# A diffusion layer in one program: fewer unread products at the start, a list that counts a half clock, another start of the buffer ring, and a new table of shifts

## The chip, the cores and the metric

The kernel runs on one core of a Trainium2 chip. Its engines are TensorE (PE, matrix products into the banks of PSUM), VectorE (DVE), ScalarE (ACT), GpSimd (POOL) and SyncE (SP, which issues nearly all DMAs). They run side by side, each working through its own list of instructions in order, and wait for each other through semaphores. The metric is the device time of one execution in microseconds (us).

## The reference

One layer over 512 latent tokens and 256 context tokens, model width 1024, all in float32:

```python
mod = silu(c) @ w_ada + b_ada                 # and the same from c_ctx, for the context
h  = rms_norm(x, g_norm1) * (1 + sc1) + sh1   # hc from ctx likewise
aq, ak, av, dq, dk, dv, dz, da, db, ga, gd = split_cols(h @ w_in)
y_attn = window_ctx_attention(q_a, k_a, v_a, k_ac, v_ac, attn_sink)
o_dc, s_cf, s_cb = bidir_delta(context inputs, zero states)    # gated delta rule, chunks of 64
o_dl, _, _ = bidir_delta(latent inputs, s_cf, s_cb)            # both directions, 8 heads of 64
y_d = rms_norm(o_dl, dn_norm_g) * silu(dz)
y = sigmoid(ga) * (y_attn @ w_br_attn) + sigmoid(gd) * (y_d @ w_br_dn)
x = x + gt1 * (y @ w_out)
x = x + gt2 * (square(relu(hm @ w_mlp1)) @ w_mlp2)             # hm: modulated norm of x
```

In a chunk of the delta rule a unit lower triangular system of 64 x 64 is solved (here by inverting its blocks), and a state of 64 x 64 per head and direction goes from chunk to chunk.

## The kernel before

Activations lie with features on the 128 partitions and tokens along the free axis, so 1024 features are 8 tiles. A product in float32 precision is mostly made of three products in a rounded format (`fp32r`): value and weight are each split into a rounded part (`hi`, ACT) and the rest (`lo`, DVE), and `mm3` (lines 331, 333, 335) adds hi*hi, hi*lo and lo*hi. Plain float32 products take two passes of PE and stand in a trace as two records.

The stages, in the order of time:

- **The front.** `ones` is a 128 x 128 tile of ones. Line 230 multiplies it with itself `NONES` times; nobody reads the result. x is loaded in four pieces (line 260); `norm_x` squares them (ACT, line 402), adds halves (DVE, 404 and 405) and sums over the features with the `ones` tile (PE, 406); then Ln and Exp on ACT (line 185) give 1/rms. Ln needs another table of functions than the Silu of c before it; line 181 loads a table. `ada` (line 249, tiles of 128 x 32) multiplies Silu(c) with 16 loads of 512 KB of `w_ada`, `columns` (267, 272, 281, 282) makes of it scale and shift of one feature tile, and `features` (339 to 341) the modulated input of that tile. Three projections begin at once on what is there (`early_x`, `early_c`). Lines 276 and 434 are further unread products, of `NWAIT` and `WARM`.
- **Projections, attention, inversion.** Weights come by DMA into a ring of `NWR` = 2 raw buffers (`wr`) and are split by lines 295 and 300 into `wh` and `wl` (`wload`, `wnext`). Softmax is at lines 657 to 746, the inversion and its last products at 894 and 993 to 1004 and, for the output, 1395 to 1407.
- **The scan** (`chain_step`, products of 64 x 64 at line 1243, DVE at 1256 to 1324), two directions in turn. Between its steps PE gets products that are independent of it: the gate tiles (line 1148) and the attention branch (1194).
- **The end of the scan.** DVE scales the output by its norm (line 1439), PE turns it back with 16 transposes (1444), DVE applies the gate (1449), lines 224 and 225 split it, and the DeltaNet branch, output projection and MLP follow in `mm3` and at line 1612.
- **The late condition weights** (`late_mod`, lines 508 and 511): 32 loads of 512 KB of `w_ada`, each summed on DVE against the row `scr_`, placed by hand between scan and MLP.

Work buffers come from one ring (`Arena`), whose pointer goes on with each `alloc`; an `alloc` that is freed at once (`NSKIP` times, line 506 before) only moves the pointer. Which buffer an `alloc` gets decides whose old readers its first writer waits for.

The order of each engine's instructions is made by a list scheduler inside the kernel (`arrange`, `Lists.run`): it goes through all instructions with a cost for each (`Step.cost`: time on the engine, time to the result), takes for each engine the ready instruction of lowest rank, and fixes the order that comes out. A rank is the place in the program plus the shifts of the table `SHIFTS` (engine or -1 for all, first, end, places). These costs set the order alone.

Of the kernel before, what the change touches and what calls it, by code (L numbers as in the profile page):

```python
# [29 lines left out]
NONES, NWAIT = 30, 8  # L30
# [7 lines left out]
NSKIP = 2  # L38
WARM = (0, 3, 3, 3, 2, 0, 0, 0)
NROWS = 2  # L40
ND1 = 3
NGD = 5
P = 128
# [8 lines left out]
HC = CH // 2  # L52
# [65 lines left out]
def tile_layer(ctx: ExitStack, tc: tile.TileContext, I: dict, out: bass.AP, dbg=None):  # L118
# [277 lines left out]
    def norm_x():  # L396
        ss = bank()
        for i in range(4):
# [7 lines left out]
            PE.matmul(ss.ap, ones, b[:, :512], start=(i == 0), stop=(i == 3))  # L406
            b.free()
        act(rx, ss.ap, AF.Ln, bias=epsc, scale=1.0 / D)
# [1343 lines left out]
class Step:  # L1752
# [39 lines left out]
    def cost(self):  # L1792

        n = self.cols
        if self.kind == "InstMatmult":
            if self.dtype.endswith("32r"):
                return (226 if n == 512 else max(60, 7 + .44 * n)), n * .44 + 175
            if self.dtype.endswith("16"):
                return 96, 240
            if self.whole:  # L1800
                return (110, 280) if self.ins.is_transpose else (max(62, 1.72 * n), max(62, 1.72 * n) + 170)
            return (142, 300) if self.tile[0] == P else (30 if self.tile[1] > HC else 19, 220)
# [78 lines left out]
class Lists:  # L1881
# [27 lines left out]
    def run(self, rank):  # L1909
# [30 lines left out]
        for _ in range(n):  # L1940
# [26 lines left out]
            else:  # L1967
                own, lag = self.cost[k]
                if e == 0:
                    words, had = words + self.words[k], words  # L1970
# [12 lines left out]
            for x in after[k]:  # L1983
                if x >= n:
                    at = end + 40
                elif eng[x] == e and not self.dma[k]:
                    at = free[e] if e == 0 else end + 10
                else:
                    at = end + note[eng[x]]
# [144 lines left out]
```

## Time and profile before

| | |
|---|---|
| median of 3 runs | 871.31 us (870.93 to 871.32) |
| the profiled execution | 871.5 us |
| its span (first to last instruction) | 869.7 us |
| PE busy | 852.3 us |
| DVE busy | 647.0 us |
| ACT busy | 498.4 us |
| DMA | 106.86 MB, mean 123 GB/s |

A row of the trace gives the start in us from the span's start, the duration in us, engine, line, operation, the tiles by the program's names (buffer numbers left out; out<-in) and, in brackets, the idle time before it and what ended it. "x16" means that many records in a row. The end of a matmul is modelled, so a row's duration is longer than its step to the next start.

### The profile page before, as it was taken

The page shows a single profiled execution, that of the slowest core. Times are in us where ns is not written, and L with a number is a line of the kernel's source. Part 1 is how long each engine was busy: PE and PEld are TensorE (multiplying, and loading weights), DVE is VectorE, ACT ScalarE, POOL GpSimd, SP SyncE. Part 2 cuts the span into 40 slices and gives each one's busy share as a digit, 9 for nine tenths or more (in the row PEclk, how much of TensorE's full clock was granted, in tenths as well). Part 3 has the DMA queues.
Part 4 walks back from the last instruction along what each step waited for, and adds up shares of the span by engine and source line. Part 5 has one row for each costly group of instructions (what it writes and reads, how often), then busy time and mean ns, then how long its engine had stood idle before and what let it go on. Part 6 is the DMA issues. An engine that isn't in the chain of part 4 may idle for free.

```text
span 869.7 us, 17973 instructions
## 1 busy us (share of the span) xinstructions
PE 852.3 (98%) x7544; PEld 712.8 (82%) x7544; DVE 647.0 (74%) x1113; ACT 498.4 (57%) x882; POOL 26.1 (3%) x42
## 2 busy tenths in 40 slices
PE   9999999999999999899999999999999999999998
PEld 6688778877777778677778899888998899889986
DVE  4865899987779997867848969993876478648741
ACT  5567875487669886587754435552555256415620
POOL 0000001010000002000000000000000000000000
PEclk9999999999999999999999999999999999999999
DMA  9924465533121236733116744743412332342031
GB/s 365 352 72 98 88 134 122 120 76 70 38 38 31 68 131 212 243 99 100 40 54 220 264 144 131 249 139 121 146 33 74 122 140 70 97 128 92 26 121 49
DMA packets 31986, 106.86 MB, mean 123 GB/s; under 512 B 4001, under 2 KB 4513, under 8 KB 31905
## 3 DMA queue, kind: packets, MB, share of 16 engines
q1 hardware_dynamic: 29600, 97.33, 33.6%
q0 software_dynamic: 2304, 8.39, 6.2%
q8 instruction: 59, 0.97, 0.5%
q14 instruction: 23, 0.18, 0.1%
HBM read 103.61 MB, written 2.10 MB: 122 GB/s over the span
## 4 chain that ended last, share of the span: by engine, by line
PE 77%; DVE 9%; ACT 6%; DMA 6%; issue 2%; SPq 0%; ACTq 0%; DVEq 0%
PE banks L331 14%; PE banks L333 14%; PE banks L335 14%; PE banks L1612 14%; PE banks L1148 7%; DMA m<-in_wada 3%; PE banks L1243 3%; PE banks L1194 3%; ACT m L185 2%; PE banks L725 1%; DVE wl L300 1%; DMA wr<-in_win 1%; PE banks L781 1%; DVE m L511 1%; DMA wr<-in_wbr 1%
## 5 line engine op out<-in xcount | busy, mean ns | idle before, releaser
L331 PE MATMUL banks<-m,wh 128*128 128x512 f32 (+1 forms) x568 | 210.7, 374 | 2.2 <-ACT m L224 1.3
L333 PE MATMUL banks<-m,wh 128*128 128x512 f32 (+1 forms) x568 | 211.2, 372 | 0.0
L335 PE MATMUL banks<-m,wl 128*128 128x512 f32 (+1 forms) x568 | 209.9, 370 | 0.1
L295 ACT ACTIVATE wh<-wr 128x1024 fp32r<-128x1024 f32 (+1 forms) x92 | 90.4, 984 | 128.3 <-PE banks L333 82.7
L331 PEld LDWEIGHTS banks<-m,wh 128*128 128x128 f32 x568 | 107.0, 189 | 20.4 <-ACT m L224 1.5
L1612 PEld LDWEIGHTS banks<-m,m 128*128 128x128 f32 x1008 | 122.2, 192 | 0.7
L335 PEld LDWEIGHTS banks<-m,wl 128*128 128x128 f32 x568 | 106.9, 188 | 19.2 <-issue 1.0
L1612 PE MATMUL banks<-m,m 128*128 128x256 f32 x1008 | 122.4, 283 | 0.0
L333 PEld LDWEIGHTS banks<-m,wh 128*128 128x128 f32 x568 | 107.1, 188 | 18.1 <-issue 0.7
L224 ACT ACTIVATE m<-m 128x512 fp32r<-128x512 f32 (+2 forms) x118 | 82.4, 721 | 66.1 <-PE banks L1612 14.9
L1148 PE MATMUL banks<-m,wh 128*128 128x512 f32 x320 | 104.1, 402 | 1.8 <-ACT m L185 1.0
L225 DVE TENSOR_TENSOR m<-m,m 128x512 fp32r<-128x512 f32 (+2 forms) x118 | 92.3, 804 | 15.5 <-ACT m L224 13.9
L300 DVE TENSOR_TENSOR wl<-wr,wh 128x1024 fp32r<-128x1024 f32 (+1 forms) x76 | 84.3, 1109 | 17.1 <-ACT wh L295 14.6
L1739 DVE SCALAR_TENSOR_TENSOR m<-banks,modT,m 128x512 f32<-128x512 f32 x32 | 24.0, 749 | 65.0 <-PE banks L335 64.9
L1148 PEld LDWEIGHTS banks<-m,wh 128*128 128x128 f32 x320 | 58.6, 188 | 14.4 <-ACT m L185 1.4
L1148 PE MATMUL banks<-m,wl 128*128 128x512 f32 x160 | 63.7, 400 | 0.4 <-DVE wl L300 0.4
L331 PE MATMUL banks<-m,m 128*128 128x256 f32 (+1 forms) x136 | 45.5, 340 | 0.4 <-ACT m L295 0.3
L333 PE MATMUL banks<-m,m 128*128 128x256 f32 (+1 forms) x136 | 45.6, 342 | 0.1
L511 DVE SCALAR_TENSOR_TENSOR m<-m,m 128x1024 f32<-128x1024 f32 x32 | 39.1, 1222 | 8.4 <-DMA m<-in_wada 8.2
L335 PE MATMUL banks<-m,m 128*128 128x256 f32 (+1 forms) x120 | 40.2, 337 | 0.0
L1243 PEld LDWEIGHTS banks<-m,m 64*64 64x64 f32 x1600 | 26.7, 134 | 12.5 <-issue 4.3
L1148 PEld LDWEIGHTS banks<-m,wl 128*128 128x128 f32 x160 | 30.0, 188 | 7.3 <-DVE wl L300 1.1
(263 smaller groups left out, 1313.7 us busy)
## 6 DMA issues: line engine op xcount, KB each, us to landing
m<-in_wada SPq DMA_DIRECT2D x48, 512.0 KB, 4.8
wr<-in_wm SPq DMA_DIRECT2D x40, 512.0 KB, 3.6
wr<-in_win SPq DMA_DIRECT2D x38, 512.0 KB, 3.7
m<-in_wm SPq DMA_DIRECT2D x24, 512.0 KB, 3.7
wl<-in_win POOLq DMA_DIRECT2D x16, 512.0 KB, 5.8
m<-in_xT SPq DMA_DIRECT2D x8, 512.0 KB, 5.9
wr<-in_wbr SPq DMA_DIRECT2D x16, 256.0 KB, 2.7
wr<-in_wout SPq DMA_DIRECT2D x8, 512.0 KB, 4.4
```

The lines of the kernel that those rows point to most:

```text
L224: A.activation(r32(hi), src, AF.Copy)
L225: (eng or V).tensor_tensor(r32(lo), src, hi, op=ALU.subtract)
L295: upper[0] = A.activation(r32(hi), raw, AF.Copy)
L300: V.tensor_tensor(r32(lo), raw, hi, op=ALU.subtract)
L331: PE.matmul(acc, w[0][:, k, :], xhi, start=(start and i == 0), stop=False)
L333: r = PE.matmul(acc, w[0][:, k, :], xlo, start=False, stop=(end and w[1] is None))
L335: r = PE.matmul(acc, w[1][:, k, :], xhi, start=False, stop=end)
L511: r = V.scalar_tensor_tensor(wa.ap, wa.ap, 0.5, scr_[0].ap, op0=ALU.mult, op1=ALU.mult, accum_out=modT[:, grp, j:j + 1])
L1148: PE.matmul(acc.ap, w[x][:, k, :], hx[k][y], start=(k == p == 0), stop=(k == KT - 1 and p == 2))
L1194: PE.matmul(pa.ap, w[x][:, j, :], r32(Q[y][:, :, j, :]), start=(j == p == 0), stop=(j == 3 and p == 2))
L1243: runs[n].append(PE.matmul(out_, w, x, start=True, stop=True).ins.name)
L1612: PE.matmul(dst, r32(self.w[w][i][:, k * P:(k + 1) * P]), xs7[x][k][j], start=(n == 0), stop=(n == 11))
```

## The change

Five things are edited:

- `NONES` goes from 30 to 16, and `norm_x` gets unread products of its own between the sums: four behind the second and two behind the third (`XWARM`).
- `NSKIP` goes from 2 to 1: the ring of buffers begins one buffer on, not two, where the late condition weights start.
- The list's costs: a PE instruction counts twice its own time before 5500 ns of the list's time (`COLD`); bf16 and small-tile products are counted shorter, whole float32 products of few columns longer, of many columns shorter.
- In the list an instruction that follows a DMA of its own queue may be issued when the queue is free, no longer only when that DMA has landed.
- `SHIFTS` has 59 new rows in place of 60.

```diff
-NONES, NWAIT = 30, 8
+NONES, NWAIT = 16, 8
-NSKIP = 2
+NSKIP = 1
 WARM = (0, 3, 3, 3, 2, 0, 0, 0)
+XWARM = (0, 4, 2, 0)
+COLD = 5500
...
     def norm_x():
         ss = bank()
+        wb_ = banks.get(512, True)
         for i in range(4):
...
-            PE.matmul(ss.ap, ones, b[:, :512], start=(i == 0), stop=(i == 3))
+            pe = PE.matmul(ss.ap, ones, b[:, :512], start=(i == 0), stop=(i == 3))
             b.free()
+            for _ in range(XWARM[i]):
+                follow(PE.matmul(wb_[:, :P], ones, ones, start=True, stop=True), pe)
+        wb_.free()
...
             if self.dtype.endswith("16"):
-                return 96, 240
+                return 80, 240
+            if self.whole and not self.ins.is_transpose:
+                return (max(224, 1.33 * n), max(224, 1.72 * n) + 170)
             if self.whole:
-                return (110, 280) if self.ins.is_transpose else (max(62, 1.72 * n), max(62, 1.72 * n) + 170)
-            return (142, 300) if self.tile[0] == P else (30 if self.tile[1] > HC else 19, 220)
+                return 110, 280
+            return (108, 400) if self.tile[0] == P else (30 if self.tile[1] > HC else 19, 220)
...
                 own, lag = self.cost[k]
                 if e == 0:
+                    if t < COLD:
+                        own, lag = 2 * own, lag + own
...
                 elif eng[x] == e and not self.dma[k]:
                     at = free[e] if e == 0 else end + 10
+                elif eng[x] == e and self.dma[x]:
+                    at = free[e]
...
 SHIFTS = (
-    (0, 2729, 2759, -37), (0, 7350, 8025, -10), (-1, 4917, 4924, 10), (0, 1436, 2436, 180), (-1, 5117, 5177, 30),
+    (-1, 2001, 2031, 120), (-1, 7610, 7760, -30), (-1, 3467, 3489, 44), (1, 2649, 2709, 30), (-1, 2779, 2979, -180),
...
```

With other costs, ranks and buffers the order differs nearly everywhere. Three places follow; a line's number is 2 to 6 higher in the changed kernel (406 is 409, 1148 is 1154, 1444 is 1450).

The front, on ACT, before: `c_cc` is the input c, `m<-m 128x1024` the squares of x, `banks,epsc` the Ln of the sum.

```order
L181 ACT_TABLE_LOAD
L402 ACTIVATE m_171<-m_123 128x1024
L402 ACTIVATE m_175<-m_123 128x1024
L402 ACTIVATE m_179<-m_123 128x1024
L402 ACTIVATE m_183<-m_123 128x512
L185 ACTIVATE m_117<-c_cc 128x8x2
L181 ACT_TABLE_LOAD
L313 ACTIVATE m_145<-wr_143 128x8x64
L185 ACTIVATE m_150<-banks,epsc 128x512
```

And in the changed kernel:

```order
L183 ACT_TABLE_LOAD
L187 ACTIVATE m_103<-c_cc 128x8x2
L183 ACT_TABLE_LOAD
L187 ACTIVATE nega<-c_prm 16x1
L405 ACTIVATE m_157<-m_109 128x1024
L405 ACTIVATE m_161<-m_109 128x1024
L405 ACTIVATE m_169<-m_109 128x1024
L405 ACTIVATE m_175<-m_109 128x512
L315 ACTIVATE m_131<-wr_129 128x8x64
L187 ACTIVATE m_136<-banks,epsc 128x512
```

The Silu of c and the second table load have moved from behind the squares to ahead of them. SP issues accordingly; before:

```order
L260 DMA m_123<-in_xT 128x1024 x4
L148 DMA m_131<-in_wada 128x1024
L148 DMA m_137<-in_wada 128x1024
L148 DMA c_cc<-in_cc 128x16
L148 DMA c_prm<-in_prm 128x188
```

In the changed kernel, to the second condition tile's loads and the first weights behind them:

```order
L150 DMA c_cc<-in_cc 128x16
L150 DMA c_prm<-in_prm 128x188
L262 DMA m_109<-in_xT 128x1024 x4
L150 DMA m_117<-in_wada 128x1024
L150 DMA m_123<-in_wada 128x1024
L311 DMA wr_129<-in_wab 128x512
L350 DMA m_110<-in_ctxT 128x1024 x2
L150 DMA m_139<-in_wada 128x1024
L150 DMA m_145<-in_wada 128x1024
L292 DMA wr_153<-in_win 128x1024
```

The two small loads have moved ahead of x, and the first projection weights (`in_win`) ahead of the third condition tile's loads; before, those weights stood three loads further back.

The inversion's last products (L894, then L900), on PE, before; `wh_4124` is the upper part of a gate tile's weights, L1243 the state's products:

```order
L1148 MATMUL banks<-m_151,wl_3810 128x512
L1243 MATMUL banks<-m_2837,m_607 64x64
L1243 MATMUL banks<-m_2837,m_606 64x64 x2
L1243 MATMUL banks<-m_2837,m_608 64x64 x2
L1148 MATMUL banks<-m_151,wh_4124 128x512 x2
L894 MATMUL banks<-m_1914,m_605 32x2x32 x4
```

In the changed kernel, the last 6 rows ahead of the same products:

```order
L1154 MATMUL banks<-m_137,wl_3801 128x512
L1154 MATMUL banks<-m_137,wh_3800 128x512 x2
L1154 MATMUL banks<-m_137,wl_3801 128x512
L1154 MATMUL banks<-m_137,wh_3800 128x512 x2
L1154 MATMUL banks<-m_137,wl_3801 128x512
L900 MATMUL banks<-m_1905,m_596 32x2x32 x4
```

The 24 products of one gate tile have moved from ahead of the last state products to behind them, and the products with the next weights (`wh_4115` here) come after the inversion's. On DVE one L1256 and one L1257 of the scan, which stood ahead of the addition L1398 that these products read, now follow it.

The end of the scan, on PE, before:

```order
L1148 MATMUL banks<-m_151,wl_5407 128x512
L1148 MATMUL banks<-m_151,wh_5406 128x512 x2
L1148 MATMUL banks<-m_151,wl_5407 128x512
L1444 MATMUL banks<-c_ident,m_5369 128x128 x16
L331 MATMUL banks<-m_5362,wh_5439 128x512
L331 MATMUL banks<-m_5362,wh_5471 128x512
```

In the changed kernel (33 products of L1154 stand between the last transpose and the first L333 of the branch):

```order
L1154 MATMUL banks<-m_137,wh_5095 128x512 x2
L1450 MATMUL banks<-c_ident,m_5360 128x128 x8
L1154 MATMUL banks<-m_137,wl_5096 128x512
L1450 MATMUL banks<-c_ident,m_5360 128x128 x8
L1154 MATMUL banks<-m_137,wh_5095 128x512 x2
L1154 MATMUL banks<-m_137,wl_5096 128x512
```

The transposes have moved ahead of 33 gate products. On DVE, in the changed kernel, the sums of late condition weights (L517) stand among the scan's last rows and just ahead of the norm's scaling (L1445, before L1439):

```order
L517 SCALAR_TENSOR_TENSOR m_5714,modT<-m_5714,m_3490 128x1024
L1327 TENSOR_TENSOR m_5254<-m_5254,banks 128x256
L517 SCALAR_TENSOR_TENSOR m_5717,modT<-m_5717,m_3490 128x1024
L1328 TENSOR_TENSOR m_4182<-m_4182,m_5254 128x256
L1327 TENSOR_TENSOR m_5265<-m_5265,banks 128x256
L1328 TENSOR_TENSOR m_4182<-m_4182,m_5265 128x256
L1330 TENSOR_REDUCE oss_2824<-m_5254 128x4
L1330 TENSOR_REDUCE oss_2824<-m_5265 128x4
L517 SCALAR_TENSOR_TENSOR m_5752,modT<-m_5752,m_3490 128x1024
L1445 TENSOR_TENSOR m_5360<-m_4182,oss_2824 128x1024 x2
```

Before, no such sum stood between the scan's last rows and L1439; they began behind it. The loads of these three and of one later sum stand on SP between those of the branch weights (`in_wbr`), where before only weights and x stood.

22 rows, old and new, of the table SHIFTS are left out of this document.

## The prediction

> **What bounds the kernel.** I read the page's first part, then PE's busy time by stage, then who ended PE's waits, then the order of time at three places.
>
> ```profile
> PE 852.3 (98%) x7544; PEld 712.8 (82%) x7544; DVE 647.0 (74%) x1113; ACT 498.4 (57%) x882; POOL 26.1 (3%) x42
> ```
>
> TensorE (PE) has something to do in 852.3 of 869.7 us, so a new order can save little more than the 17 us that are left, and it pays only where PE stands idle. The stages below (stretch, its length, PE busy, PEld, DVE, ACT, POOL, granted clock, DMA share, GB/s) tell where that is.
>
> ```profile
> 12.90:25.00 12.10, 10.80 (x97) 7.05 (x96) 7.92 (x17) 7.83 (x14) 0.00 (x0) 1.00 1.03 419
> ...
> 340.00:380.00 40.00, 36.73 (x823) 29.20 (x822) 30.09 (x54) 26.11 (x52) 6.24 (x12) 1.00 0.58 196
> ...
> 560.00:865.00 305.00, 305.00 (x1821) 273.17 (x1820) 195.01 (x275) 130.84 (x167) 0.00 (x0) 1.00 0.31 100
> ```
>
> From 560 us on PE is never idle (305.00 of 305.00): nothing there can be won by order. In the front 1.30 us are idle while the loads run at 419 GB/s, and between 340 and 380 us 3.27 us. The waits of PE (who waited for whom: us, times, longest) name the same places:
>
> ```profile
> PE banks L331 <- ACT m L224: 1.3, 1, 1.3
> PE banks L1004 <- issue: 1.2, 1, 1.2
> PE banks L894 <- DVE m L1398: 0.8, 1, 0.8
> ```
>
> All are single waits of about 1 us, so each moved piece below is worth about 1 us or nothing.
>
> **The front.** PE, ACT, DVE and SP in the first 16 us:
>
> ```profile
> 1.06 8.43 PE L230 MATMUL banks<-ones 128*128 128x128 f32 x60 [1.06 <-DVE ones L195]
> 9.33 3.60 PE L406 MATMUL banks<-m,ones 128*128 128x512 f32 x8
> ...
> 4.41 1.06 ACT L402 ACTIVATE m<-m 128x1024 f32<-128x1024 f32 x1 [2.38 <-DMA m<-in_xT]
> 11.62 0.22 ACT L185 ACTIVATE m<-c_cc 128x16 f32<-128x16 f32 x1 [2.11 <-DMA c_cc<-in_cc]
> 11.86 1.28 ACT L181 ACT_TABLE_LOAD   x1
> 13.15 0.63 ACT L313 ACTIVATE m<-wr 128x512 fp32r<-128x512 f32 x1
> 13.69 0.67 ACT L185 ACTIVATE m<-banks,epsc 128x512 f32<-128x512 f32 x1
> ...
> 10.13 0.69 DVE L405 TENSOR_TENSOR m<-m 128x512 f32<-128x512 f32 x1
> 15.77 0.75 DVE L339 SCALAR_TENSOR_TENSOR m<-m,modA,m 128x512 f32<-128x512 f32 x1
> ...
> 0.75 1.81 SPq L260 DMA_DIRECT2D m<-in_xT  x4
> 4.04 0.45 SPq L148 DMA_DIRECT2D c_prm<-in_prm  x1
> ```
>
> The unread products are two passes each (60 records for 30). Their pace by stretch:
>
> ```profile
> 0.00:4.20 4.20, 3.13 (x15) 3.14 (x16) 1.00 0.57 187
> 4.20:9.30 5.10, 5.10 (x48) 5.10 (x46) 1.00 0.99 390
> ```
>
> About 0.21 us a pass up to 4.2 us and 0.11 after it: a half-speed start that the granted-clock column (1.00) does not show. The 14 products left out are 28 passes at 0.11, 3.1 us of PE; the six put between the sums add 12 passes, 1.3 us. Neither is worth its length. PE would finish 16 products at about 4.2 + 18 x 0.11 = 6.2 us, and then waits for the sums, whose last input DVE makes ready at 10.13 + 0.69 = 10.8 us. That input now comes later: SP issues the small loads of c and of the parameters ahead of the four x loads, two issues of 0.45 us, so x starts up to 0.9 us later (at least the 0.25 us that 102 KB take at 419 GB/s, an estimate from that row). Last sum: ready at 11.1 to 11.7, its two passes 0.9 us (a quarter of the 3.60), done at 12.0 to 12.6 instead of 9.33 + 3.60 = 12.9. The gain lies on ACT: the load of the Ln table, 1.28 us, waited for c (11.62) and stood ahead of the split at 13.15 and the Ln at 13.69; now both Silu and table come before the first square, in time that ACT idled (2.38 us). Ln then starts at about 12.9, bound by sum and weight split: 0.8 us earlier. The ends are 1.3 us earlier (the whole table load) and 0.9 us later (all x late, and the split's own load with it). What reaches the end is less: after 25 us the same loads feed PE, the stream begins 0.25 to 0.9 us later, and the loads of the third condition tile now stand behind half a megabyte of weights. I take **-0.3 us**, near the middle of the two ends, on the side of the shorter ACT chain.
>
> [...]
>
> **The end of the scan.** Rows of DVE, PE and ACT at 443 to 457 us:
>
> ```profile
> 443.05 2.36 DVE L1439 TENSOR_TENSOR m<-m,oss 128x1024 f32<-128x1024 f32 x2 [0.65 <-ACT oss L185]
> ...
> 453.06 0.39 PE L1148 MATMUL banks<-m,wl 128*128 128x512 f32 x1
> 453.29 1.91 PE L1444 MATMUL banks<-c_ident,m 128*128 128x128 f32 x16
> 454.49 1.28 ACT L181 ACT_TABLE_LOAD   x1
> 456.47 1.00 PE L331 MATMUL banks<-m,wh 128*128 128x512 f32 x3 [1.27 <-ACT m L224]
> ```
>
> The transposes (L1444) are PE's last work before the branch products (L331) that need them, with DVE, a table load and ACT's split between: 1.27 us idle. Now 33 gate products (L1148, 0.23 us each, as from 453.06 to the next start: 7.5 us) stand behind the transposes, more than the chain from 453.29 to 456.47 needs. The transposes come 7.5 us sooner, at about 445.8; their input is ready at 443.05 + 2.36 = 445.4, with 0.4 us to spare. I take the whole wait, **-1.3 us**; the other end is the second rival's.
>
> **The last products of the inversion.** Around 369 us:
>
> ```profile
> 368.13 0.73 PE L1148 MATMUL banks<-m,wh 128*128 128x512 f32 x2 [0.78 <-ACT wh L295]
> 368.63 0.42 DVE L1256 TENSOR_TENSOR m<-banks,eg 128x256 f32<-128x256 f32 x1
> 368.97 0.68 DVE L1398 TENSOR_TENSOR m<-m,banks 128x512 f32<-128x512 f32 x1
> 369.70 1.48 PE L894 MATMUL banks<-m,m 64*32 64x64 f32 x128 [0.84 <-DVE m L1398]
> ```
>
> PE waits 0.78 us for a weight split and 0.84 us for DVE. Now 24 gate products (5.4 us) stand between the last state product and these products, and the weights waited for come after them. Between 1.6 us (both waits gone) and nothing (DVE sets the time, PE just waits once): on DVE one L1256 and one L1257, 0.42 us each, no longer stand ahead of L1398, so I take **-0.8 us**.
>
> **Changes of tile form.** A trip from full tiles into smaller ones and back costs time of its own:
>
> ```profile
> 397.71 1.63 PE L1243 MATMUL banks<-m,m 64*64 64x64 f32 x96
> 399.27 0.51 PE L1148 MATMUL banks<-m,wl 128*128 128x512 f32 x1
> 399.70 0.69 PE L1243 MATMUL banks<-m,m 64*64 64x64 f32 x32
> 400.33 0.73 PE L1148 MATMUL banks<-m,wh 128*128 128x512 f32 x2
> ```
>
> The run of 96 takes 1.56 us to the next start, that of 32 0.63, so 32 more cost 0.47 and the way out 0.16; the way in is 0.43 - 0.23 = 0.20. PE makes 59 such trips now, 56 before: three at 0.36 are 1.1 us. Two lie in the front, where PE idles anyway: **+0.7 us**, ends 0.3 and 1.1.
>
> The buffer ring begun one buffer on changes which old reader each load waits for; no row prices it, and what could be late by it is in the second rival. The list's own costs and its half clock cost nothing: they are worked out before the run and act through the order alone.
>
> **Sum.** -0.3 - 1.3 - 0.8 + 0.7 = -1.7 us, against the profiled execution's 871.5: 869.8. The median of the runs is 0.2 below that execution, so 869.6 us. Ends: -1.3 - 1.3 - 1.6 + 0.3 = -3.9 (867.4); with the second rival's loss and late x, some 5 us longer.
>
> **Rivals.**
> First, no change: the waits move instead of going. For it: PE's wait of 1.2 us at L1004 is "issue", no buffer's and no engine's, and the others of the list sit in softmax and scan, chains of ACT and DVE which PE only visits. The front's gain would be eaten by the later stream, and 369 us stays DVE's. Then -0.3 to +0.3: 871.3 us.
>
> Second, slower: DVE at the end of the scan. Four loads of the late condition weights (512 KB) now stand on SP at the scan's end, between the branch weights, and three of their sums on DVE ahead of L1439. Their group on the page (busy, mean ns, idle before):
>
> ```profile
> L511 DVE SCALAR_TENSOR_TENSOR m<-m,m 128x1024 f32<-128x1024 f32 x32 | 39.1, 1222 | 8.4 <-DMA m<-in_wada 8.2
> ```
>
> Three are 3.7 us, and nine waits for such loads made 8.2 us, 0.9 each. DVE idles there for want of input (0.65 us ahead of L1439 alone), which hides part, and 0.4 us is PE's slack. It decides once L1439 ends more than 0.4 + 1.3 us behind PE's last gate product ahead of the transposes. If DVE is 3.4 us late, PE idles 3.0 us: -1.7 + 1.3 + 3.0 = +2.6, 873.9 us. Against it: the first two of the sums stand between scan rows that wait for PE.
>
> Third, a small part of the slower chance: with 32 passes in place of 60 the half clock lasts into the sums. Each of their eight passes would take 0.9 instead of 0.45, but the first six wait for x anyway: at most 0.9 us. [...]
>
> **Chances.** The forecast 0.50 (its own range 868.0 to 870.8), no change 0.28, slower 0.22. About 0.2% (1.7 us, below 869.6 or above 873.0) is what a measurement can tell here. The forecast lies at that edge: 0.32 of it is faster, 0.18 the same. The first rival gives 0.06, 0.20 and 0.02, the second 0.02 the same and 0.20 slower. Together: faster 0.38, same 0.40, slower 0.22. Range 866.8 to 873.8.
>
> **What would show it.** Right: Ln in the front near 12.9 us and the first feature on DVE near 15.0; no wait over 0.3 us at the first branch product after the scan, and the transposes starting within 0.5 us of L1439's end; the two waits at 369 us summing to 0.8 or less. Wrong: L1439 waiting behind a late condition sum, a wait at the transposes, first features later than 15.8, or new waits of 1 us in softmax (200 to 300 us), which this sum holds at no change.

## The result, and the profile after

The change made the kernel slower, outside the predicted range:

| | before | changed |
|---|---|---|
| median of 4 runs | 871.32 us (870.93 to 871.46) | 879.61 us (876.98 to 881.57) |
| ratio, 95% interval | | 1.0092 (1.0073 to 1.0111) |
| the profiled execution, its span | 871.5, 869.7 us | 880.24, 878.5 us |
| PE idle, up to its last product | 13.56 us | 18.51 us |

PE's idle time here is what is left of a stretch when the union of PE's records is taken out; the 3.8 us behind PE's last product, the same in both, are not in it. The busy line and the stages of the changed kernel, in the columns of the prediction:

```profile
PE 856.1 (97%) x7528; PEld 713.3 (81%) x7528; DVE 646.6 (74%) x1113; ACT 495.2 (56%) x882; POOL 26.0 (3%) x42
```

```profile
12.90:25.00 12.10, 10.53 (x90) 6.09 (x89) 7.59 (x13) 6.99 (x11) 0.00 (x0) 1.00 1.03 419
340.00:380.00 40.00, 35.03 (x905) 27.58 (x903) 30.06 (x51) 23.48 (x43) 5.18 (x10) 0.96 0.66 213
...
560.00:865.00 305.00, 305.00 (x1818) 272.67 (x1818) 203.17 (x286) 133.35 (x172) 0.00 (x0) 1.00 0.32 107
```

The last stage is as full as before, so the loss lies ahead of it. Of the 8.8 us of span, 5.0 are new idle time and 3.8 more busy time. The stretch from 340 to 380 us, the place of the forecast's -0.8, is the worst: 35.03 us busy in place of 36.73, and a granted clock of 0.96. By stage, PE idle in us:

| us from the start | 0-25 | 25-180 | 180-300 | 300-335 | 335-385 | 385-440 | 440-460 | 460-560 |
|---|---|---|---|---|---|---|---|---|
| before | 2.4 | 1.5 | 4.3 | 0.0 | 3.6 | 0.4 | 1.3 | 0.2 |
| changed | 3.9 | 0.9 | 5.5 | 0.9 | 5.9 | 0.0 | 0.2 | 1.3 |

PE's longest waits (us, times, longest) name a new first place:

```profile
PE banks L1000 <- issue: 2.5, 1, 2.5
PE banks L900 <- DVE m L1404: 1.9, 1, 1.9
PE banks L409 <- DVE m L408: 1.1, 1, 1.1
```

The prediction had 1.2 us of "issue" at L1004 in a fence and used it only as a wait that the change would not touch; the "issue" is 2.5 us now. It has also moved: L1004 of before is L1010 here, and L1000 was L994, another run of the inversion's small products. The second row is the wait before the inversion's last products, which was to shrink. Four places follow.

**The stop at 345 us.** PE's rows, then what moved on the DMA queues from 344.5 to 345.5 us, then two stretches behind the stop:

```profile
344.12 0.19 PE L1010 MATMUL banks<-m,m 32*32 32x32 f32 x1
...
346.85 0.21 PE L1000 MATMUL banks<-m,m 32*32 32x32 f32 x1 [2.48 <-issue]
```

```profile
q8 instruction: 1, 0.02, 5.5%
```

```profile
347.72:351.13 3.41, 3.41 (x10) 2.76 (x9) 1.23 (x2) 0.00 (x0) 1.88 (x4) 0.50 0.86 267
351.13:354.54 3.41, 3.41 (x16) 2.77 (x16) 0.43 (x1) 1.50 (x2) 0.19 (x1) 1.00 0.62 228
```

PE stops in the midst of 32 x 32 products that wait for nothing on another engine. One packet of 0.02 MB arrives in the stop on a queue of its own, labelled "instruction", and PE goes on after it: PE has run out of program (the counts at "Where the stops stand" below bear this out). After the stop the granted clock is 0.50 for one window of 3.41 us: 10 products fall in it, 16 in the next.

**The inversion's last products.** DVE and PE, then the late condition sums on DVE from 360 to 385 us, changed and before:

```profile
373.28 1.22 DVE L517 SCALAR_TENSOR_TENSOR m<-m,m 128x1024 f32<-128x1024 f32 x1
...
375.33 1.22 DVE L517 SCALAR_TENSOR_TENSOR m<-m,m 128x1024 f32<-128x1024 f32 x1
376.47 0.68 DVE L1404 TENSOR_TENSOR m<-m,banks 128x512 f32<-128x512 f32 x1
377.21 1.49 PE L900 MATMUL banks<-m,m 64*32 64x64 f32 x128 [1.88 <-DVE m L1404]
```

```profile
L517 DVE SCALAR_TENSOR_TENSOR m<-m,m 128x1024 f32<-128x1024 f32 x7 | 8.6, 1221 | 4.5 <-DMA m<-in_wada 4.4
```

```profile
L511 DVE SCALAR_TENSOR_TENSOR m<-m,m 128x1024 f32<-128x1024 f32 x4 | 4.9, 1226 | 1.5 <-DMA m<-in_wada 1.5
```

Two sums stand close ahead of the addition L1404 that PE waits for; seven fall in the stretch, where four did, one of them only with its end.

**The end of the scan.**

```profile
451.60 1.22 DVE L517 SCALAR_TENSOR_TENSOR m<-m,m 128x1024 f32<-128x1024 f32 x1
...
452.75 2.35 DVE L1445 TENSOR_TENSOR m<-m,oss 128x1024 f32<-128x1024 f32 x2
```

```profile
454.25 1.03 PE L1450 MATMUL banks<-c_ident,m 128*128 128x128 f32 x8
...
476.09 0.50 PE L333 MATMUL banks<-m,wh 128*128 128x512 f32 x1 [0.62 <-ACT wh L297]
```

The transposes start within 0.3 us of their half of L1445 and the wait of 1.27 is gone. But a wait for a weight split opens 20 us later.

**The front.** Rows of the changed kernel on PE, ACT, DVE and SP, its two first stretches, and two rows of before that the prediction did not show:

```profile
1.07 6.36 PE L232 MATMUL banks<-ones 128*128 128x128 f32 x32 [1.07 <-DVE ones L197]
13.93 1.07 PE L251 MATMUL banks<-m,m 128*32 128x256 f32 x16
...
6.74 1.06 ACT L405 ACTIVATE m<-m 128x1024 f32<-128x1024 f32 x1 [2.32 <-DMA m<-in_xT]
10.68 0.63 ACT L405 ACTIVATE m<-m 128x512 f32<-128x512 f32 x1 [0.19 <-DMA m<-in_xT]
14.36 0.67 ACT L187 ACTIVATE m<-banks,epsc 128x512 f32<-128x512 f32 x1
...
16.59 0.75 DVE L341 SCALAR_TENSOR_TENSOR m<-m,modA,m 128x512 f32<-128x512 f32 x1
...
1.67 1.86 SPq L262 DMA_DIRECT2D m<-in_xT  x4
```

```profile
0.00:4.20 4.20, 3.13 (x14) 3.13 (x15) 0.82 (x9) 2.78 (x3) 0.21 (x4) 1.00 0.42 111
4.20:9.30 5.10, 3.96 (x22) 3.34 (x20) 1.07 (x3) 2.32 (x4) 0.00 (x0) 1.00 0.92 343
```

```profile
8.88 0.63 ACT L402 ACTIVATE m<-m 128x512 f32<-128x512 f32 x1 [0.18 <-DMA m<-in_xT]
...
12.86 1.07 PE L249 MATMUL banks<-m,m 128*32 128x256 f32 x16
```

x is issued 0.92 us later and its last piece is squared 1.80 us later: until 4.2 us 111 GB/s move in place of 187. The first condition product starts 1.07 later, Ln 0.67, the first feature 0.82; its 16.59 lies past the 15.8 that the prediction named as a sign of being wrong.

### The profile page after: what moved, and what is told of

It reads as the page before. It is cut to its first block, busy times and chain, and to the rows that moved or that the text cites. A ratio compares the mean times of both kernels' runs of the same rounds, so it can differ in the third digit from the quotient of the medians.

```text
span 878.5 us, 17937 instructions
## 1 busy us (share of the span) xinstructions
PE 856.1 (97%) x7528; PEld 713.3 (81%) x7528; DVE 646.6 (74%) x1113; ACT 495.2 (56%) x882; POOL 26.0 (3%) x42
## 5 line engine op out<-in xcount | busy, mean ns | idle before, releaser
L333 PE MATMUL banks<-m,wh 128*128 128x512 f32 (+1 forms) x568 | 211.6, 375 | 0.9 <-ACT wh L297 0.9
L1618 PE MATMUL banks<-m,m 128*128 128x256 f32 x1008 | 128.7, 283 | 0.0
L1618 PEld LDWEIGHTS banks<-m,m 128*128 128x128 f32 x1008 | 125.2, 191 | 1.1
L333 PEld LDWEIGHTS banks<-m,wh 128*128 128x128 f32 x568 | 107.1, 189 | 19.0 <-ACT wh L297 1.8
L1154 PE MATMUL banks<-m,wh 128*128 128x512 f32 x320 | 106.4, 406 | 1.2 <-ACT m L187 0.6
L1154 PEld LDWEIGHTS banks<-m,wh 128*128 128x128 f32 x320 | 59.4, 191 | 14.1 <-ACT m L187 1.2
L1154 PE MATMUL banks<-m,wl 128*128 128x512 f32 x160 | 65.0, 407 | 0.2 <-DVE wl L302 0.2
L333 PE MATMUL banks<-m,m 128*128 128x512 f32 (+1 forms) x136 | 45.0, 342 | 1.2 <-ACT m L297 0.8
L335 PE MATMUL banks<-m,m 128*128 128x512 f32 (+1 forms) x136 | 45.1, 341 | 0.8 <-DVE m L343 0.6
L517 DVE SCALAR_TENSOR_TENSOR m<-m,m 128x1024 f32<-128x1024 f32 x32 | 38.6, 1217 | 6.8 <-DMA m<-in_wada 6.7
L337 PE MATMUL banks<-m,m 128*128 128x512 f32 (+1 forms) x120 | 39.9, 336 | 0.0
L1154 PEld LDWEIGHTS banks<-m,wl 128*128 128x128 f32 x160 | 30.3, 190 | 7.1 <-DVE wl L302 0.4
```

Of the source, the lines that this page charges most:

```text
L333: PE.matmul(acc, w[0][:, k, :], xhi, start=(start and i == 0), stop=False)
L335: r = PE.matmul(acc, w[0][:, k, :], xlo, start=False, stop=(end and w[1] is None))
L337: r = PE.matmul(acc, w[1][:, k, :], xhi, start=False, stop=end)
L517: r = V.scalar_tensor_tensor(wa.ap, wa.ap, 0.5, scr_[0].ap, op0=ALU.mult, op1=ALU.mult, accum_out=modT[:, grp, j:j + 1])
L1154: PE.matmul(acc.ap, w[x][:, k, :], hx[k][y], start=(k == p == 0), stop=(k == KT - 1 and p == 2))
L1618: PE.matmul(dst, r32(self.w[w][i][:, k * P:(k + 1) * P]), xs7[x][k][j], start=(n == 0), stop=(n == 11))
```

## The experiments

For these the order that the list gives each engine was written out row by row, so that single rows could be moved with all else in place. Ratios are to the kernel before, run beside on the same chip, with 95% intervals. Moved rows are shown with + and - on the engine named.

**The changed kernel, order written out**, the control for what follows:

```diff
-SHIFTS = ( ... )
+ORDER = ( ... )      # the order that SHIFTS gave
```

> The changed kernel itself, its order written out as a list, beside the others on the same chip. Both theories: 878 to 881 us, and a half-clock stretch of 3.41 us behind the stop at 344 us in most runs.

879.33 us (877.43 to 881.03), 1.0080 (1.0063 to 1.0097): the same kernel. The stop is there again, and behind it 24 gate products:

```profile
344.85 0.21 PE L1000 MATMUL banks<-m,m 32*32 32x32 f32 x1 [2.48 <-issue]
```

```profile
345.67:352.63 6.96, 6.96 (x30) 5.56 (x24) 1.74 (x3) 1.60 (x2) 2.06 (x4) 0.75 0.75 244
```

**12 gate products ahead of the third run of inversion products** (the second of L999 and L1000), so that PE's program is used up more slowly there:

```diff
 L1010 MATMUL banks<-m_3499,m_3537 32x32
+L1154 MATMUL banks<-m_137,wl_3435 128x512      (12 in all, hi and lo)
 L999 MATMUL banks<-m_3496,m_797 32x32
 ...
 L1000 MATMUL banks<-m_3500,m_797 32x32
-L1154 MATMUL banks<-m_137,wl_3435 128x512      (12 in all)
```

> The changed kernel with one edit on PE: 12 of the gate products (L1154) that stand behind the long stop at 344 us now stand ahead of the last run of inversion products (L999, L1000), so that two dense runs of small products no longer follow each other directly. Theory A (PE ran out of instructions there: the 16 KB block that it needed began to arrive at 344.57, behind 512 KB loads; and the 3.41 us at half clock followed from that stop): the 2.48 us stop shrinks to under 0.5, no half-clock stretch follows near 350 us, and the time falls by 2.0 (stop alone) to 3.7 us (stop and half clock), to some 876 us, with less spread between the runs than the 4.6 us of the changed kernel. Theory B (PE waits there for something else, or the work behind it is late anyway): the stop only moves, the time stays at 879 to 880 us.

878.11 us (876.46 to 880.79), 1.0070 (1.0056 to 1.0084). The stop did not go, it came in pieces (340 to 385 us):

```profile
PE banks L1009 <- issue: 1.7, 1, 1.7
PE banks L1249 <- issue: 1.5, 1, 1.5
PE banks L1154 <- issue: 1.2, 1, 1.2
```

**Two condition sums behind the addition** (DVE):

```diff
-L517 SCALAR_TENSOR_TENSOR m_4035,modT<-m_4035,m_3490 128x1024
 L1403 TENSOR_TENSOR m_3889<-m_793,banks 64x4x2x32
 L1262 TENSOR_TENSOR m_4191<-banks,eg 128x256
+L1404 TENSOR_TENSOR m_794<-m_794,banks 128x512
+L517 SCALAR_TENSOR_TENSOR m_4035,modT<-m_4035,m_3490 128x1024
 L517 SCALAR_TENSOR_TENSOR m_4038,modT<-m_4038,m_3490 128x1024
-L1404 TENSOR_TENSOR m_794<-m_794,banks 128x512
```

> The changed kernel with one edit on DVE: two sums of the late condition weights (L517, 1.22 us each) that stand between the inversion's last DVE steps and L1404 now stand behind L1404. Theory A (PE's wait of 1.88 us at 377 us is these sums): the wait falls to under 0.3 us and the time by 1.6 to 1.9 us. Theory B (PE waits once in any case, for the copies on ACT or the next sum): the wait moves to the next step of the scan, and the time falls by less than 0.5 us.

878.26 us (876.16 to 881.2), 1.0077 (1.0059 to 1.0095). The wait at L900 went from 1.88 to 0, and waits of 0.8 us for a weight split and 0.4 us for ACT took its place: no gain that shows. This run's stop was as long, 2.36 us, but the edge between two clock windows divided it into 0.77 and 1.59 us (the control's into 0.48 and 2.00), and the same 24 gate products ran at full clock:

```profile
345.48 0.21 PE L1000 MATMUL banks<-m,m 32*32 32x32 f32 x1 [2.36 <-issue]
```

```profile
346.30:351.69 5.39, 5.39 (x32) 4.42 (x24) 1.85 (x5) 1.68 (x3) 2.07 (x4) 1.00 0.93 321
```

5.39 us against 6.96 in the control: the half clock after the stop cost 1.6 us there. It came behind a window that held 2.00 us of the stop, and not behind one that held 1.59.

**The whole front of before**: 30 unread products, none between the sums, every engine's order as before up to 45 us, the changed order behind.

```diff
-NONES, NWAIT = 16, 8
+NONES, NWAIT = 30, 8
-XWARM = (0, 4, 2, 0)
+XWARM = (0, 0, 0, 0)
```

> The changed kernel, but its first 45 us are those of the kernel before: 30 unread products, none between the sums, x ahead of c and of the parameters, and each engine's order as before up to there; behind it the changed order. Theory A (the new front costs, since x lands 1.8 us later and PE reaches the first ada product 1.07 us later): the time falls by 1 to 2 us against the changed kernel. Theory B (the front's delay is taken up by the loads until 45 us): the time stays within 0.5 us. Theory C (nearly all of the loss is in the front): the time falls by 5 us or more.

875.0 us (874.65 to 875.6), 1.0038 (1.0026 to 1.0050). About half of the loss is gone, far more than the front's own delay. Waits from 340 to 385 us:

```profile
PE banks L1154 <- ACT m L187: 2.2, 2, 1.6
PE banks L1010 <- issue: 1.8, 2, 1.2
```

The stop is shorter and at another row, though no row there was moved. The same kernel again:

> The same kernel as the run with the front of before, as the control for the next two on one chip. All theories: 874.6 to 875.6 us.

876.08 us (874.16 to 877.23, ten runs), 1.0037 (1.0025 to 1.0049). In this execution the two stops were 0.76 and 1.14 us, at the same two places.

**The number of unread products alone**: the edit above, with the changed order everywhere else.

> The changed kernel's order throughout, but with 30 unread products at the start and none between the sums: eight float32 products more, so that every later PE instruction stands 32 places further on in its 16 KB block. Theory A (the stop at 344 us depends on where the blocks end): the stop shrinks from 2.48 us to about 1.2 and the half clock behind it goes, as in the kernel with the whole front of before; the front stays as late, or 0.5 us later, and the time falls by 2 to 3 us. Theory B (the front's lateness alone set what followed): the time stays at 879 to 881 us with the stop in its place.

877.15 us (875.12 to 878.56), 1.0052 (1.0035 to 1.0068); the stop is 1.41 us, at L1010 as with the whole front of before. **The order of the front alone**: 16 and 6 products, but every engine's order up to 45 us as before.

> The changed program with its 16 unread products and the six between the sums, but each engine's order up to 45 us is that of the kernel before: x ahead of c and of the parameters on SP, the squares ahead of the Silu and the second table load on ACT. Theory A (the front's loss is the late x, that is the order of the loads): the front ends 1.2 to 2.6 us earlier and the time falls by as much against the changed kernel, while the stop at 344 us and the half clock behind it stay, since PE's instructions stand in the same places of their 16 KB blocks. Theory B (the loss is the fewer products, whose half clock lasts until 5 to 6.5 us): less than 0.5 us.

879.52 us (878.57 to 880.45), 1.0085 (1.0069 to 1.0101): nothing gained by the loads' order with few products, and the stop is 2.97 us. So the products account for about 2.2 us of the loss (879.33 - 877.15; the two intervals overlap by a little), and the load order counts only together with them.

**Gate products in three places**: 8, 16 and 8 between the three runs of inversion products, in the changed kernel.

```diff
-L1154 MATMUL banks<-m_137,wl_3318 128x512      (8, ahead of the first run)
 L999 MATMUL banks<-m_3496,m_796 32x32
 ...
+L1154 MATMUL banks<-m_137,wl_3318 128x512      (8, behind it; likewise 16 and 8)
```

> The changed kernel with the gate products around 344 us spread: 8 of the 28 ahead of the first dense run of inversion products now stand behind it, 16 of the 24 behind the third now ahead of it, 8 of the 18 behind the fourth ahead of it. Theory A (PE's instructions come at one 16 KB block, 128 product records, per some 4.8 us here, since one fetch at a time takes about 2.4 us to begin, 0.9 to move and 1.4 until PE goes on; three dense runs of 128 in 3.4 us outrun that): with 4 to 5 us between the runs all stops called issue in this stretch together shrink from 3.9 us (2.48, 0.55 and 0.90 at L1249) to under 1.0, no half clock follows, and the time falls by 3 to 4.5 us. Theory B (one stop shifted only, as with the first trial of 12 products): no change.

877.19 us (875.55 to 880.12), 1.0061 (1.0043 to 1.0078): no "issue" at 340 to 360 us, but 1.15 us for ACT (L1001) and 1.15 and 0.68 at L900. That is 2.1 us below the control (877.19 against 879.33), as much as the products alone won, with intervals that overlap in the same way. **The same on top of the front of before:**

> The changed kernel with the first 45 us of before, and the gate products around 344 us spread (8, 16 and 8 moved); DVE as in the changed kernel. Theory A (the block stops are paid in full): the two stops called issue, 1.2 + 0.6 us, go and the time falls by 1.2 to 1.8 us against 875.0 to 876.1, to about 874. Theory B (the inversion's chain on DVE and ACT at 366 to 376 us sets the time whenever PE comes earlier): PE's waits there grow by as much as the stops gave, and the time stays at 875 to 876.

875.88 us (874.37 to 876.99), 1.0044 (1.0029 to 1.0058): no gain over the front alone. With the stops gone, 340 to 385 us waits elsewhere:

```profile
PE banks L1154 <- ACT m L187: 2.8, 2, 1.8
PE banks L1009 <- ACT m L1001: 1.1, 1, 1.1
```

**On top of that, condition sums moved** (DVE; the first kernel):

```diff
-L517 SCALAR_TENSOR_TENSOR m_4040,modT<-m_4040,m_3498 128x1024     (and m_4043, m_4046; m_3905 two rows later)
 ...
+L1404 TENSOR_TENSOR m_802<-m_802,banks 128x512
+L517 SCALAR_TENSOR_TENSOR m_4040,modT<-m_4040,m_3498 128x1024
+L517 SCALAR_TENSOR_TENSOR m_4043,modT<-m_4043,m_3498 128x1024
 L517 SCALAR_TENSOR_TENSOR m_4046,modT<-m_4046,m_3498 128x1024
-L1404 TENSOR_TENSOR m_802<-m_802,banks 128x512
```

The second kernel also moves a weight split on ACT behind the one that PE waits for in softmax; the third is the first with the last two sums put four rows further down, behind the weight split `wl_4124`.

```diff
 L776 ACTIVATE m_2404<-banks,c_prm 128x512
+L226 ACTIVATE m_2397<-banks 128x1024
 L297 ACTIVATE wh_2446<-wr_2444 128x1024
-L226 ACTIVATE m_2397<-banks 128x1024
```

> That kernel (order of before up to 45 us, changed order behind it) with two further edits: the gate products around 344 us spread as in the earlier trial (8, 16 and 8 moved), and on DVE four condition sums (those at 366.57, 369.84, 373.28 and 375.33 in the changed kernel) and one gate step (L1159) behind the inversion steps L1401, L1403 and L1404 which they stood ahead of. Theory A (the block stops, 1.18 + 0.62 us, and the sums, PE waits of 1.57 and 1.60 us at 366 and 373 us, are most of what is left): 3 us less, about 872, level with the kernel before. Theory B (PE's waits move to the next step of the inversion or to weight splits): 874 to 875.

> As the run before, with one weight split on ACT (L297, 1.06 us, at 230.44 in the changed kernel) behind the split L226 for which PE waits at 232.47. Theory A: PE's waits of 1.01 and 0.47 us there fall by 0.9 to 1.4 us together and the time by as much, below the kernel before. Theory B (the second wait or the scan behind softmax takes it): less than 0.3 us.

> As that, and on DVE the condition sum at 366.57 behind L1401, the gate step at 370.99 behind L1403, the sum at 369.84 behind L1404, and the two at 373.28 and 375.33 behind the weight split L302 that the next gate products need. Theory A (sums and stops are most of the 3 us that are left): no wait over 1.3 us at 366 to 380 us, and 872 to 873.5. Theory B (the later sums hold up the loads behind them on SP, and a split is late again): 875 or more.

879.53 us, 1.0083 (1.0069 to 1.0097); 878.3 us, 1.0071 (1.0056 to 1.0087); 877.85 us, 1.0077 (1.0062 to 1.0092). All three lost. Against the second run of the front of before, the first reached the products at L900 1.3 us sooner (372.26 against 373.53) and then met a sum whose load came late, ahead of a weight split on DVE; the third reached them 2.8 us sooner and gave it back twice:

```profile
378.56 0.80 PE L1154 MATMUL banks<-m,wl 128*128 128x512 f32 x1 [4.15 <-DVE wl L302]
```

```profile
376.02 0.45 PE L1249 MATMUL banks<-m,m 64*64 64x64 f32 x10 [1.59 <-DVE m L1263]
...
387.19 0.93 PE L1249 MATMUL banks<-m,m 64*64 64x64 f32 x48 [2.56 <-ACT m L1288]
```

The softmax split gained 0.2 us at most at its place.

**The kernel before, its own stop filled**: 8 gate products moved ahead of a run of inversion products, and then with one sum and two weight splits moved too.

```diff
 L1148 MATMUL banks<-m_151,wl_3527 128x512
+L1148 MATMUL banks<-m_151,wh_3526 128x512 x2    (8 in all)
 L1003 MATMUL banks<-m_3504,m_3734 32x32
 ...
 L1004 MATMUL banks<-m_3508,m_3734 32x32
-L1148 MATMUL banks<-m_151,wh_3526 128x512 x2    (8 in all)
```

> The kernel before with one edit on PE: 8 of the gate products (L1148) that stand behind the run of L1003 and L1004 products now stand ahead of it. Theory A (the 1.18 us that PE stood still there was the wait for a block of instructions, too): the stop goes and the time falls by 0.8 to 1.2 us below the kernel before, to about 870.3. Theory B (another wait takes its place): no change, 871.3.

> The kernel before with four edits of the same kinds: 8 gate products ahead of the run that stopped at 350.44 us; on DVE the condition sum at 365.26 behind L1398; on ACT the weight split at 367.04 ahead of five state updates (L1299), and the one at 229.38 behind the split L224 that softmax waits for. Theory A (the stop of 1.18 us, the waits of 0.78 and 0.84 us at 368 and 370 us and part of the 0.89 at 231.8 go together, since the split that took the place of the first stop in the earlier trial now comes sooner): 1.5 to 2.8 us less than the kernel before, 869 to 870.5. Theory B (waits move): within 0.5 us of it.

872.01 us, 1.0000 (0.9991 to 1.0008), and 872.3 us, 1.0003 (0.9993 to 1.0012). The first removes the stop of 1.18 us and puts a wait for a weight split in its place; in the second that wait is 1.5 us, with another 1.5 for ACT (L1282):

```profile
PE banks L1148 <- ACT wh L295: 2.4, 1, 2.4
```

**The kernel before with 22 unread products:**

```diff
-NONES, NWAIT = 30, 8
+NONES, NWAIT = 22, 8
```

> The kernel before in its own order with one edit: 22 unread products at the start in place of 30, as many as the changed kernel has in all. Theory A (fewer instructions ahead put the ends of the 16 KB blocks elsewhere in the dense runs of the inversion, so the edit costs at 350 us and not at the start): the front stays within 0.2 us; PE's stop of 1.18 us at 350.44 changes by 1 us or more, most likely to 2 us or more, since the place at which a fetch is asked for moves by 16 records, which among gate products is 3.6 us; the time rises by 1 to 3 us. Theory B (unread products that end before x is there have no price and no use): the time stays at 871 to 872 us and the stop at 1.2.

873.19 us (871.16 to 874.93), 1.0008 (0.9998 to 1.0019). The stop stayed at 1.27 us: in this order eight products fewer did not lengthen it, so that expectation missed. The profiled execution had three half windows (from 14.84 us and, two in a row, from 369.82 us) where that of before had none, and 6 of its 12 runs had a mean clock of 0.996 or less, against 2 of 17 of the kernel before.

**Where the stops stand.** The traces of all these runs settle what the stops are. An execution has 59 instruction packets of 16 KB (0.97 MB in all) for its 7528 or 7544 products, so a block of program holds some 128 products with their weight loads. Number PE's records (weight loads, products, semaphore and drain records) from the first: all 31 idle times of PE that the profile calls issue, in 16 executions, end at the 193rd or 194th record of a group of 256, that is at the same edge of a block. How long PE stops goes with what the block before that edge holds:

| executions | unread products | gate products in the block | block used up in | stop behind it, at 341 to 351 us |
|---|---|---|---|---|
| changed, control, two sums behind, front order alone | 22 | 0 | 1.29 us | 2.36 to 2.97 us |
| front of before (twice), products alone | 30 | 4 | 2.5 us | 0.76 to 1.41 us |
| before | 30 | 4 | 2.5 us | 1.18 us |
| before with 22 unread products | 22 | 4 | 2.5 us | 1.27 us |

In the changed order, eight unread products fewer move the blocks' edges 16 product records on. The edge then falls behind the four gate products that stand between the first two runs, and the next block holds 32 x 32 products alone. In the order of before the same shift stays inside a run: 106 of its products stand ahead of the stop in place of 90, and the block still holds its four gate products. So eight unread products fewer went with a longer stop where the edge passed slower work (2.36 to 2.97 us against 0.76 to 1.41), and not where it stayed in the same run (1.27 against 1.18).

**The order of before up to 180, 300 or 400 us on the changed kernel's ring**, meant as a ledger of where the loss is made:

```diff
-NSKIP = 2
+NSKIP = 1
```

> The kernel before (30 unread products, no others between the sums) with the changed ring start, its own order up to 180 us and the changed order behind it (4 steps had to move for the other buffers). With the run that had the order of before up to 45 us, 875.0 us. Theory A (the loss is spread over front, softmax and inversion: PE's idle time was 0.97 us less than before from 100 to 180 us in the changed order): 875.5 to 876.5. Theory B (all that is left lies behind 300 us): 875.0.

> The same with the order of before up to 300 us (33 steps had to move). Theory A (softmax and the scan's begin from 180 to 300 us cost 1.2 to 1.5 us of idle time in the changed order): 1.2 to 1.5 us below the run with 180. Theory B: as the run with 180.

> The same with the order of before up to 400 us (34 steps had to move), so that of the changed order only the end of scan, the branches and the MLP are left. Theory A (the inversion from 300 to 400 us carries 3 us): 871 to 872 us, level with the kernel before; the changed end of the scan, whose wait of 1.27 us went, is given back by 0.5 + 0.6 us of new waits from 460 to 560 us. Theory B (the end of the scan is a net gain): 870 to 870.7. Theory C (the loss is behind 400 us): 873 or more.

877.15 us, 1.0064 (1.0042 to 1.0086); 884.2 us, 1.0140 (1.0117 to 1.0163); 892.75 us, 1.0231 (1.0214 to 1.0249). The last two are slower than either parent. On the other ring 4, 33 and 34 rows had to move because their buffers have other readers, and the order of before fits it badly: from 180 to 300 us, ahead of the place where the orders join, PE idles 8.5 us in the second and the third kernel, where it idled 4.3 in the kernel before and 5.5 in the changed one. In the third kernel, 260 to 340 us:

```profile
PE banks L1031 <- ACT m L1036: 3.8, 1, 3.8
PE banks L1031 <- DVE m L747: 2.0, 1, 2.0
```

So this is no ledger. It shows that this order, found for one ring start, does not carry to the other; what the join of the two orders costs by itself isn't separated.

## Why the prediction was wrong, point by point

The forecast was 1.7 us less; the measured change is 8.3 us more.

**The front, -0.3.** Wrong: about +1 us. The step "x starts up to 0.9 us later" was mis-sized: x started 0.92 later but was squared 1.80 to 2.33 later, since the first 4.2 us moved 111 GB/s where before had moved 187. That ate the 1.28 us of the table load, which did leave ACT's path. The third rival's half clock was thought over by 4.2 us: here 25 of the 32 passes ran at half speed, 0.21 us each, until 6.39 us, and the products ended at 7.43, not 6.2. That did not go with the number of products: over the 20 profiled executions the half-speed start ended between 4.16 us (the kernel before) and 7.27, with few and with many unread products alike.

**The products as "neither is worth its length".** This is the largest failure that a run isolates. Leaving them out was priced at the time that they take in the front. Putting them back, alone, won 2.2 us, and the front's rows account for about 1 us of what the whole front won (879.33 less 876.08 or 875.0: 3.3 to 4.3 us). The stop at 345 us went from 2.5 to 1.2 and 1.4 us with them, with no row changed there, and half clock became rarer: 3 of 5 runs with the products alone, and 5 of 15 with the whole front of before, had a mean clock of 0.998 or less, against 4 of 5 of the control. What the prediction lacked is that the number of products ahead set where PE's blocks of program ended 330 us later (eight products fewer moved the ends 16 product records on); the counts at "Where the stops stand" show it, and show why eight products fewer in the kernel before left its stop as it was.

**The end of the scan, -1.3.** Right as a step: wait gone (1.27 to 0.15 us idle), input ready in time, and the three sums ahead of L1445 cost nothing to be seen. But 1.1 us came back as waits from 460 to 560 us. "What is late next" was not asked there.

**The inversion, -0.8.** Wrong in sign: 0.78 + 0.84 became 1.88 us, and 0.9 of issue behind, at another block's edge. The failed step is "DVE sets the time, PE just waits once", with only the two scan rows counted on DVE. The sums of the late condition weights stood there too: the second rival's mechanism, at another place than it was looked for. The experiment that moved two of them removed that wait, and won nothing.

**Changes of form, +0.7.** Not separable: PE is 1.6 us busier than before even with the old front, and no run broke that down.

**"It sits at L1004 and is issue".** The row was read as a wait that no change of order touches. It was the edge of a block of program, and a change of PE's order or of the number of products ahead of it can move slow or fast work to that edge: the stop in this stretch grew by 1.3 us, the most of all waits, and brought 1.6 us of half clock behind it. The sum had no term for it.

**"New waits in softmax, held at no change".** 1.3 us more idle from 180 to 300 us and 0.9 more from 300 to 335, with 0.6 less ahead of that. Why is open.

**The rivals' prices.** The second rival gave 873.9 as the slow end; the median was 5.7 us above it, because it was one mechanism and several came together. The stated range, up to 873.8, did not even hold that price, nor the "some 5 us longer" of the sum.

How the loss divides. The table sorts runs by the mean clock granted to PE:

| | runs at clock 1.000 | other runs |
|---|---|---|
| before, beside the second run of the old front | 870.72 to 872.93 | up to 874.07 (0.995) |
| changed, old front (both times) | 874.16 to 876.51 | up to 877.23 (0.998) |
| changed | 876.98 | 878.98 (0.998), 880.24 (0.997), 881.57 (0.994) |

The medians of the runs at 1.000 are 871.3, 874.8 and 876.98 us (of the changed kernel that is one run). By them half clock is worth up to 2.6 us of the 8.3 (879.61 - 876.98; by the control's one run at 0.999, 879.33 - 877.88, 1.5), the old front another 2.2 (876.98 - 874.8), and 3.5 us remain that no run removed. Of the 4.0 us by which the first profiled execution with the old front is longer than that of before, 2.4 are idle time (4.2 more from 180 to 385 us, 1.8 less elsewhere) and 1.6 are busy time that nothing here explains. In the idle part PE waits for DVE and ACT: where a stop was filled or a sum moved, the next wait in the same 50 us took its place. The rows suggest where that begins, untested:

```profile
331.02 12.35 SPq L514 DMA_DIRECT2D m<-in_wada  x3
344.77 2.06 SPq L292 DMA_DIRECT2D wr<-in_win  x2
347.62 1.77 SPq L514 DMA_DIRECT2D m<-in_wada  x2
```

```profile
336.57 4.14 DVE L989 STREAM_TRANSPOSE m<-m 128x1024 f32<-128x1024 f32 x2
340.63 1.17 DVE L517 SCALAR_TENSOR_TENSOR m<-m,m 128x1024 f32<-128x1024 f32 x1
```

```profile
332.86 1.25 DVE L511 SCALAR_TENSOR_TENSOR m<-m,m 128x1024 f32<-128x1024 f32 x1
```

In the changed kernel the first late sum in this stage comes at 340.63, behind four long transposes; in the kernel before (last fence) one came at 332.86, and ten had begun by 360 us against six. Meanwhile SP is held for 12.35 us over three loads whose buffers are not free, and seven sums crowd into 360 to 385 us. No version found here beat the kernel before.

## What to carry to other kernels

A wait called "issue" inside a dense run of small products was here a supply limit: find the instruction packets beside it, count PE's records to see where its blocks end, and price any change in the number of earlier instructions, unread ones too, by what it does to the block that ends there. A wait taken away was no gain here where the next producer had no time to spare (the 1.88 us at L900 went, and waits of 0.8 and 0.4 us took its place), so ask of each engine in the stretch what else the new order has put on it. An order, the count of instructions ahead of it and the start of its buffer ring were found together and are judged together: pieces of one put into another cost up to 21 us.

## What the runs showed of the hardware

- PE's program came in blocks of 16 KB on a DMA queue (q8: 59 packets, 0.97 MB, for 7544 products), so some 128 products each. A run of 128 products of 32 x 32 took 1.1 us, and a block of nothing else was used up in 1.29 us, faster than the next one came: in the kernel before and the changed one, successive fetches from 335 to 360 us stood 4.3 us or more apart, and PE went on 2.3 to 2.8 us after the fetch beside a stop began. The stops of all executions were 0.3 to 3.0 us, and all stood at record 193 or 194 of 256.
- The granted clock changed at the edges of windows of 3.41 us: in the changed kernel its record starts at 6.39 us and shows full clock for 100.0 windows, half from 347.72 us for one, and full for 154.0; in the kernel before it starts at 4.16 us and shows full clock for 254.0. Over the full-clock windows of all profiled executions, a window in which PE idled 1.93 us or more was followed by half clock 11 times of 11 (2.48 us in the changed kernel, 2.00 in the control); with 1.47 to 1.88 us 10 times of 19 (with 1.49 at 229.14 us in the front order alone it was, with 1.88 at 375.03 us in the changed kernel it was not); with less never.
